# RWKV scan without zero-padded operands, with the gram in a two-bank tile, and modulations computed 512 columns at a time

## The chip, the core and the metric

The kernel runs on one core of one Trainium2 chip. The metric is the device time of one execution in microseconds (us). The profile names the engines PE (TensorE matmuls), PEld (TensorE weight loads), DVE (VectorE), ACT (ScalarE), POOL (GpSimd) and SP (SyncE, which issues all of this kernel's DMAs). "L529" is line 529 of the kernel before.

## The reference

Two layers, each a token mixer and a convolutional FFN, over 1024 latent and 256 context tokens of width 1024. The mixer has four groups of heads; two matter here. The RWKV-7 group is a bidirectional linear recurrence with four heads of 64 in each direction:

```python
def rwkv_scan(r, w, k, v, a, b, state):
    def step(s_mem, inp):
        rt, wt, kt, vt, at, bt = inp
        sa = jnp.einsum('bhvk,bhk->bhv', s_mem, at)
        s_new = s_mem * wt[:, :, None, :] + sa[..., None] * bt[:, :, None, :] + vt[..., None] * kt[:, :, None, :]
        return s_new, jnp.einsum('bhvk,bhk->bhv', s_new, rt)
```

The modulations are `mod = silu_c @ ada_w[l] + ada_b[l]` for two vectors (latent and context): six groups of 1024 columns per layer, each contracted over 1024 rows of weights.

## The kernel before, in words

A layer projects its input, runs Hyena and retention, and then has a stage in which three things run side by side: the RWKV scan (`rwkv` and its helpers), the mLSTM (`mlstm`) and the modulations (`ada_steps`). When all three have ended, `load_wo` brings the output projection's weights, `mix_out` normalises, gates and projects, and the FFN follows. All instructions of the stage are traced in program order and then arranged by a planner that models their times; each engine and the SP queue afterwards run their own lists strictly in order. The trace order is two steps of the scan, then the whole mLSTM with a step of the modulations at each of its 17 or 19 stations, then the rest of the scan.

The scan takes ten steps per layer. A step handles one tile of 128 tokens forward and one backward (index d), each of two chunks of 64 tokens (c), with four heads as two pairs f and two halves q of the 128 partitions.

- `rwkv_prep` (L470 to L542) loads its operands (L479 to L484), computes decays (L492 to L511), scales keys and queries (L514 to L526), forms the gram of keys with queries (L529), masks it into G (L530), copies or transposes its diagonal blocks into NB (L535, L536), and transposes the keys (L540, copied at L541). For the gram, AR holds the queries with zeros in the other head's partitions: a matmul contracts over all 128 partitions and gives 256 columns for both heads.
- `rwkv_inverse` (L545 to L558) inverts 32x32 triangular blocks: LM is a transposed, replicated copy of NB (L550), X starts at L551, and 31 rounds of a multiply (L557) and an add (L558) follow, one half of the columns on POOL, the other on DVE.
- `rwkv_tail` (L561 to L591) transposes X (L565, L569, L571), completes the 64x64 inverse with two batches of 32x32 matmuls (L577 to L586) and writes XT (L570, L590, L591).
- `rwkv_chain` (L594 to L638) is the serial part: for each chunk i and direction d a round of b0 = G V + AR S (L611, L612), U (L614), XT U (L615), its copy into VSA (L617, half on ACT and half on DVE), and the new state (L621, L622, L624). Then come the outputs y (L629, L630) and their copy or sum into YF (L636, L637). SV holds the state in one half of the partitions and the values in the other; V is loaded into VSA and SV both.

`rwkv` calls them so that step s of the chain stands between the inverse and the tail of step s+1, and the prep of step s+2 follows. G and bt have three buffers, AR three, XT, VSA and SV two, LM, X, NB and most of prep's tiles one. PSUM has two banks each for cbank (chain and tail), dbank (gram and key transposes) and mbank (mLSTM and modulations), one for ybank and one for pbank (L492). `ada_steps` works in units of 256 columns, two column groups of 128, whose weights come in four tiles through two buffers; `ada_out` copies the sums to SBUF on DVE (L940), transposes them (L941) and adds the bias (L944). `group_norm` sends YF to the DRAM tensor yw (L659), and `mix_out` reads it back at L1138.

Of the kernel before, what the change touches and what calls it, by code (L numbers as in the profile page):

```python
# [429 lines left out]
def rwkv(K,l,pv,last,p1,p2,p3):  # L430
# [8 lines left out]
    TWA=p1.tile([128,2,2,128],F32,name="TWA"); nc.gpsimd.memset(TWA,0.0)  # L439
# [4 lines left out]
    for a in range(2):  # L444
        r=slice(64,128) if a==0 else slice(0,64); o=slice(0,64) if a==0 else slice(64,128)
# [24 lines left out]
def rwkv_prep(K,C,s):  # L470
    nc=K.nc; act=nc.scalar.activation; tt=nc.vector.tensor_tensor; mm=nc.tensor.matmul; ts=nc.vector.tensor_scalar
    p=C['p']; p3=C['p3']; pv=C['pv']; bank=K.dbank; A=ALU
    rkk=p3.tile([128,2,8,128],F32,tag="rkk",name="rkk")
# [972 lines left out]
```

## Time and profile before

| what | value |
|---|---|
| median of 3 runs | 4259.41 us (4256.86 to 4265.3) |
| the profiled execution's own time | 4269.9 us |
| its span, first to last instruction | 4268.0 us |
| mean granted TensorE clock | 0.940 of full speed |
| busy shares of the span | PE 93%, DVE 63%, ACT 33%, POOL 23% |

The page gives shares over the whole span. The stage of the change is two stretches of it, one per layer, about 770 to 1239 us and 2948 to 3391 us; the long stretches around them are projections and FFN, where PE is busy almost without a break. A busy time of PE counts overlapping modelled durations, so within the stage the starts of its instructions tell more than the share.

### The profile page before, as it was taken

How to read it: one execution, taken by the hardware profiler on the slowest of the kernel's cores; microseconds unless marked ns; L12 is line 12 of the kernel's file. 1: busy time of each engine (PE TensorE's matmuls, PEld its weight loads, DVE VectorE, ACT ScalarE, POOL GpSimd, SP SyncE). 2: the span in 40 equal slices, each digit the busy share in tenths (PEclk: the TensorE clock that was granted, in tenths of full speed). 3: DMA queues.
4: the chain of work that ended last, by engine and by line, in shares of the span. 5: the costliest groups of instructions: out<-in, count | busy, mean ns of one | idle time of the engine just before them, and what ended most of it. 6: DMA issues, size and time to landing. Idle time of an engine off the chain costs nothing.

```text
span 4268.0 us, 65334 instructions
## 1 busy us (share of the span) xinstructions
PE 3956.8 (93%) x24976; PEld 3210.9 (75%) x24976; DVE 2672.2 (63%) x5412; ACT 1416.9 (33%) x2855; POOL 979.7 (23%) x2158
## 2 busy tenths in 40 slices
PE   5999999699979999999997999996899899999998
PEld 3878877566668888888884688885666678888886
DVE  5655665789769444444449555676888684444447
ACT  4433343554344211211123433344544342112121
POOL 3320023466512000000021221024666320000002
PEclk6999999789989999999998999997899699999999
DMA  4235444343343111111113235553332431111112
GB/s 166 74 102 177 149 153 122 112 143 116 122 160 119 45 40 34 41 40 35 37 35 124 82 91 154 169 162 114 122 115 84 136 114 55 48 41 55 45 50 99
DMA packets 477138, 414.16 MB, mean 97 GB/s; under 512 B 48827, under 2 KB 443284, under 8 KB 474010
## 3 DMA queue, kind: packets, MB, share of 16 engines
q1 hardware_dynamic: 476826, 409.99, 31.0%
q8 instruction: 197, 3.23, 0.3%
q14 instruction: 115, 0.94, 0.1%
HBM read 323.65 MB, written 86.25 MB: 96 GB/s over the span
## 4 chain that ended last, share of the span: by engine, by line
PE 52%; DVE 11%; DMA 3%; issue 2%; POOL 1%; ACT 1%; SPq 0%; ACTq 0%; DVEq 0%; POOLq 0%
PE bank L1022 9%; PE bank L1023 9%; PE bank L1024 9%; PE dbank L1022 6%; PE dbank L1023 6%; PE dbank L1024 6%; DVE bst L983 1%; DMA xt<-x 1%; DVE facc L1205 1%; PE bank L186 1%; PE bank L187 1%; DMA wst<-in_w_out 1%; PE dbank L529 0%; DVE facc L1206 0%; DVE facc L1274 0%
## 5 line engine op out<-in xcount | busy, mean ns | idle before, releaser
L1022 PE MATMUL dbank<-uh,wh 128*128 128x512 f32 (+1 forms) x2120 | 765.3, 370 | 8.8 <-ACT tmpB L398 5.7
L1023 PE MATMUL dbank<-ul,wh 128*128 128x512 f32 (+1 forms) x2120 | 761.2, 368 | 0.0
L1016 DVE TENSOR_TENSOR wl<-wst,wh 128x1024 fp32r<-128x1024 f32 x146 | 185.5, 1272 | 491.9 <-ACT wh L1015 367.3
L1024 PE MATMUL dbank<-uh,wl 128*128 128x512 f32 (+1 forms) x2120 | 480.6, 367 | 0.0
L1022 PEld LDWEIGHTS dbank<-uh,wh 128*128 128x128 f32 x2120 | 401.4, 189 | 85.0 <-ACT tmpB L398 6.1
L1023 PEld LDWEIGHTS dbank<-ul,wh 128*128 128x128 f32 x2120 | 401.6, 189 | 68.9 <-issue 1.1
L1024 PEld LDWEIGHTS dbank<-uh,wl 128*128 128x128 f32 x2120 | 365.9, 188 | 70.5 <-issue 1.5
L1264 DVE TENSOR_TENSOR facc<-facc,bank 128x512 f32<-128x512 f32 x324 | 221.8, 686 | 205.1 <-PE bank L1024 205.1
L1022 PE MATMUL bank<-uh,wh 128*128 128x512 f32 (+1 forms) x920 | 334.9, 372 | 4.5 <-ACT uh L1010 4.5
L1233 POOL MEMSET fz<- 128x1 f32 x132 | 7.2, 98 | 1433.6 <-DVE fc L1248 1433.6
L1023 PE MATMUL bank<-ul,wh 128*128 128x512 f32 (+1 forms) x920 | 335.1, 372 | 0.8 <-DVE ul L1011 0.8
L1022 PE MATMUL bank<-wdh,gh 128*128 128x512 f32 x792 | 314.9, 400 | 17.9 <-DVE facc L1278 8.7
L1023 PE MATMUL bank<-wdl,gh 128*128 128x512 f32 x792 | 310.5, 392 | 1.0 <-DVE wdl L1016 1.0
L1024 PE MATMUL bank<-wdh,gl 128*128 128x512 f32 x792 | 248.1, 392 | 0.0
L1015 ACT ACTIVATE wh<-wst 128x1024 fp32r<-128x1024 f32 x146 | 154.8, 1060 | 238.1 <-PE dbank L1023 168.4
L1015 ACT ACTIVATE wdh<-wst 128x1024 fp32r<-128x1024 f32 x46 | 48.8, 1062 | 529.4 <-PE bank L1024 427.7
L558 POOL TENSOR_TENSOR XL<-XL,lt 128x48 f32<-128x48 f32 (+26 forms) x620 | 204.4, 330 | 47.7
L557 POOL TENSOR_TENSOR lt<-LM,XL 128x48 f32<-128x48 f32 (+26 forms) x620 | 187.1, 302 | 119.4 <-ACT XL L551 45.0
L1024 PE MATMUL bank<-uh,wl 128*128 128x512 f32 (+1 forms) x920 | 211.9, 372 | 0.0
L1022 PEld LDWEIGHTS bank<-uh,wh 128*128 128x128 f32 x920 | 174.1, 190 | 36.1 <-ACT uh L1010 5.6
L1023 PEld LDWEIGHTS bank<-ul,wh 128*128 128x128 f32 x920 | 174.2, 189 | 31.9 <-DVE ul L1011 1.7
L1022 PEld LDWEIGHTS bank<-wdh,gh 128*128 128x128 f32 x792 | 149.7, 189 | 59.4 <-DVE facc L1278 14.9
(476 smaller groups left out, 8132.3 us busy)
## 6 DMA issues: line engine op xcount, KB each, us to landing
wst<-in_ffn_w_up SPq DMA_DIRECT2D x88, 512.0 KB
adaw<-in_ada_w SPq DMA_DIRECT2D x160, 256.0 KB
wst<-in_w_in SPq DMA_DIRECT2D x58, 512.0 KB
wst<-in_ffn_w_down SPq DMA_DIRECT2D x46, 512.0 KB
df<-in_c_F SPq DMA_DIRECT2D x10, 1344.0 KB
xt<-x SPq DMA_DIRECT2D x26, 512.0 KB
df<-in_c_I SPq DMA_DIRECT2D x8, 1344.0 KB
rkk<-wrk SPq DMA_DIRECT2D x10, 1024.0 KB
```

Source lines behind the costliest of these rows:

```text
L186: mm(dst_re,F[:,i],pre(slot),start=True,stop=False); mm(dst_re,F[:,i+1],pim(slot),start=False,stop=True)
L187: mm(dst_im,F[:,i],qim(slot),start=True,stop=False); mm(dst_im,F[:,i+2],qre(slot),start=False,stop=True)
L557: e.tensor_tensor(out=t_,in0=LM[:,j,j+1:32].unsqueeze(2).to_broadcast([128,n,m]),in1=X[h][:,j:j+1,0:m].to_broadcast([128,n,m]),op=A.mult)
L558: e.tensor_tensor(out=X[h][:,j+1:32,0:m],in0=X[h][:,j+1:32,0:m],in1=t_,op=A.add)
L983: for h in range(2): nc.vector.bn_stats(out=st[:,h],in_=x[h])
L1015: k.nc.scalar.activation(out=h,in_=st,func=ACTF.Copy)
L1016: k.nc.vector.tensor_tensor(out=lo,in0=st,in1=h,op=ALU.subtract)
L1022: mm(ps,lh,rh,start=(i==0),stop=False)
L1023: mm(ps,lh,rl,start=False,stop=False)
L1024: for i,((lh,ll),(rh,rl)) in enumerate(pairs): mm(ps,ll,rh,start=False,stop=(i==n-1 and more is None))
L1205: for o,i,gg in zip([y[:,h] for h in hs],x,[g[:,h] for h in hs]) if parts else [(y,x,g)]: stt(out=o,in0=i,scalar=m,in1=gg,op0=ALU.subtract ...
L1264: else: tt(out=d,in0=d,in1=ps,op=ALU.add)
```

## The change

The zero halves of AR, TWA and XT go, and with them the memsets that made them. The gram is formed per head from 64 partitions, the two heads into the two banks of one PSUM tile (xbank, one buffer); the key transposes move from dbank to pbank. The state has its own tile S, both halves in one update; V is no longer loaded twice. AR S, XT U and AR S in y become 64x64 matmuls; the identity pass for the state is one 128x128 matmul instead of four. All copies at L591 and L617 are on ACT, the products rho (L601) on POOL. y stands on the partitions of its head, so the copy into YF is one instruction per direction, and the DRAM tensor yw has another order, which `mix_out` undoes with eight small DMAs instead of one. Modulations use a stationary operand padded to 32 columns, units of 512 columns (four column groups) and eight buffers of weights, and one ACT copy of the sums instead of two (four at the start of the program) on DVE. dbank is gone in the stage; `load_rows` uses mbank there.

```diff
-    TWA=p1.tile([128,2,2,128],F32,name="TWA"); nc.gpsimd.memset(TWA,0.0)
+    TWA=p1.tile([128,2,128],F32,name="TWA")
...
-    AR=[p1.tile([128,2,2,2,2,2,64],F32,name="AR%d"%i) for i in range(3)]
-    for t in AR: nc.gpsimd.memset(t[64:128,:,:,:,0],0.0); nc.gpsimd.memset(t[0:64,:,:,:,1],0.0)
-    XT=[p1.tile([128,2,4,128],F32,name="XT%d"%i) for i in range(2)]
+    AR=[p1.tile([128,2,2,2,2,64],F32,name="AR%d"%i) for i in range(3)]
+    XT=[p1.tile([128,2,4,64],F32,name="XT%d"%i) for i in range(2)]
...
-        for X in (VSA,SV):
-            for o,n in PAIR: nc.sync.dma_start(X[r,q,o].rearrange("p d c f e -> p d (c f e)") if o is ALL else X[r,q,o].rearrange("p c f e -> p (c f e)"),K.D['wv'][n,q].rearrange("n p c x -> p n (c x)") if o is ALL else K.D['wv'][n,q].rearrange("p c x -> p (c x)"))
+        r=slice(q*64,q*64+64); X=VSA
+        for o,n in PAIR: nc.sync.dma_start(X[r,q,o].rearrange("p d c f e -> p d (c f e)") if o is ALL else X[r,q,o].rearrange("p c f e -> p (c f e)"),K.D['wv'][n,q].rearrange("n p c x -> p n (c x)") if o is ALL else K.D['wv'][n,q].rearrange("p c x -> p (c x)"))
...
-                o=slice(d*256+ft*128,d*256+ft*128+128); mm(bb[i][:,o],C['W2'][:,o],C['TWA'][:,i,d],start=True,stop=True)
+                r=slice(i*64,i*64+64); o=slice(d*256+ft*128,d*256+ft*128+128); mm(bb[i][:,o],C['W2'][r,o],C['TWA'][r,d],start=True,stop=True)
...
-        for q in range(2):
-            r=slice(q*64,q*64+64)
-            (nc.gpsimd if d==0 else nc.vector).tensor_tensor(out=ar[r,d,:,:,q,0],in0=v4(rkk[r,d,6:8]),in1=Wp[r],op=A.mult)
-            tt(out=ar[r,d,:,:,q,1],in0=v4(rkk[r,d,0:2]),in1=W[r],op=A.mult)
-        for a in range(2): tt(out=bk[:,d,:,:,a],in0=bk[:,d,:,:,a],in1=Wi,op=A.mult)
-        for c in range(2):
-            b=bank()
-            for f in range(2): mm(b[:,f*256:f*256+256],bk[:,d,f,c].rearrange("p a t -> p (a t)"),ar[:,d,f,c].rearrange("p q a t -> p (q a t)"),start=True,stop=True)
-            tt(out=G[:,d,c].rearrange("p f q t -> p (f q) t"),in0=b.rearrange("p (a t) -> p a t",a=4),in1=C['rmask'][:,d].unsqueeze(1).to_broadcast([128,4,128]),op=A.mult)
+        (nc.gpsimd if d==0 else nc.vector).tensor_tensor(out=ar[:,d,:,:,0],in0=v4(rkk[:,d,6:8]),in1=Wp,op=A.mult)
+        tt(out=ar[:,d,:,:,1],in0=v4(rkk[:,d,0:2]),in1=W,op=A.mult)
+        bka=bk[:,d].rearrange("p f c a t -> p (f c) a t"); tt(out=bka,in0=bka,in1=Wi.rearrange("p f c t -> p (f c) t").unsqueeze(2).to_broadcast([128,4,2,64]),op=A.mult)
+        b=K.xbank(); b=[b[:,i] for i in range(2)]
+        for cf in range(4):
+            for q in range(2):
+                r=slice(q*64,q*64+64); c,f=cf//2,cf%2
+                mm(b[q][:,cf*128:cf*128+128],bk[r,d,f,c].rearrange("p a t -> p (a t)"),ar[r,d,f,c].rearrange("p a t -> p (a t)"),start=True,stop=True)
+        for q in range(2): tt(out=G[:,d,:,:,q].rearrange("p c f t -> p (c f) t"),in0=b[q].rearrange("p (a t) -> p a t",a=4),in1=C['rmask'][:,d].unsqueeze(1).to_broadcast([128,4,128]),op=A.mult)
...
-        b=bank()
+        b=K.pbank()
...
-        nc.vector.tensor_copy(out=XT[hi,1,:,lo],in_=bv[hi])
+        act(out=XT[hi,1,:,0:32],in_=bv[hi],func=ACTF.Copy)
...
-        for d in range(2): tt(out=rho[:,i,d],in0=io[:,1,d,:,i^d],in1=(Pn if i else P)['io'][:,0,d,:,d if i else 1-d],op=A.mult)
+        for d in range(2): nc.gpsimd.tensor_tensor(out=rho[:,i,d],in0=io[:,1,d,:,i^d],in1=(Pn if i else P)['io'][:,0,d,:,d if i else 1-d],op=A.mult)
...
-                for r,q in HQ: mm(b0[r,f*64:f*64+64],ar[:,d,f,ch,q,0],SV[:,d,ch,q,f],start=False,stop=True)
+                for q in range(2): mm(b0[H[1-q],f*64:f*64+64],ar[H[q],d,f,ch,0],S[H[q],d,ch,f],start=False,stop=True)
...
-            for f in range(2): mm(b1[:,f*64:f*64+64],XT[:,d,ch*2+f],U[:,f],start=True,stop=True)
+            for f in range(2):
+                for r in H: mm(b1[r,f*64:f*64+64],XT[r,d,ch*2+f],U[r,f],start=True,stop=True)
...
-            act(out=VSA[0:64,d,ch,0],in_=bv[0:64],func=ACTF.Copy); nc.vector.tensor_copy(out=VSA[64:128,d,ch,1],in_=bv[64:128])
+            for r,q in ((H[0],1),(H[1],0)): act(out=VSA[r,d,ch,q],in_=bv[r],func=ACTF.Copy)
...
-                    for r,q in HQ: mm(b2[r,f*64:f*64+64],K.ident[:,r],SV[:,d,ch,q,f],start=True,stop=False)
+                mm(b2,K.ident,S[:,d,ch].rearrange("p f e -> p (f e)"),start=True,stop=False)
...
-                for r,q in HQ: tt(out=SN[r,d,cn,q],in0=bv[r],in1=rho[r,i,d].unsqueeze(2).to_broadcast([64,2,64]),op=A.mult)
+                tt(out=SN[:,d,cn],in0=b2.rearrange("p (f e) -> p f e",f=2),in1=rho[:,i,d].unsqueeze(2).to_broadcast([128,2,64]),op=A.mult)
...
+            for d in range(2):
+                c=i^d
+                for f in range(2):
+                    for q in range(2): mm(y[H[q],d,c,f],G[:,d,c,f,q,64:128],VSA[:,d,c,q,f],start=True,stop=False)
+                    for q in range(2): mm(y[H[q],d,c,f],ar[H[q],d,f,c,1],S[H[q],d,c,f],start=False,stop=True)
...
-    for j in range(G): nc.vector.tensor_copy(out=ab[32*j:32*j+2],in_=ps[32*j:32*j+2,0:n])
+    nc.scalar.activation(out=ab,in_=ps[:,0:n],func=ACTF.Copy)
...
-        for h in range(4):
-            t=pool.tile([128,2,256],F32,tag="adaw",name="adaw",bufs=2); w[u].append(t)
+        for q in range(8):
+            t=pool.tile([128,512],F32,tag="adaw",name="adaw",bufs=8); w[u].append(t)
...
-                for j in range(2): nc.tensor.matmul(ps[32*j:32*j+2,0:128],k.sc[:,q],w[u][q//2][:,q%2,j*128:j*128+128],start=(q==0),stop=(q==7))
+                for j in range(4): nc.tensor.matmul(ps[32*j:32*j+32,0:128],sc[:,q],w[u][q][:,j*128:j*128+128],start=(q==0),stop=(q==7))
...
+            for t in range(2):
+                for c_ in range(2):
+                    for q in range(2): nc.sync.dma_start(yv[c_*64:c_*64+64,t,q],yw[t,c_,q])
...
-        psum(k,cbank=2,ybank=1,pbank=1,dbank=2,mbank=2)
+        psum(k,cbank=2,ybank=1,pbank=1,xbank=-1,mbank=2)
```

## Rows read from the trace of the kernel before

**Rows 1.** The page: its head.
```profile
span 4268.0 us, 65334 instructions
```

**Rows 2.** Windows, both stages: length, busy PE PEld DVE ACT POOL, PEclk, DMA, GB/s.
```profile
770.00:1239.00 469.00, 392.51 (x4570) 293.40 (x4570) 386.38 (x1156) 220.49 (x591) 251.61 (x693) 0.86 0.42 128
2948.00:3391.00 443.00, 367.53 (x4094) 281.34 (x4095) 373.44 (x1095) 204.68 (x572) 249.42 (x689) 0.81 0.37 114
```

**Rows 3.** Source view of L550: ns min/median/max, first to last start; each layer.
```profile
L550 DVE STREAM_TRANSPOSE LM<-NB x10: 1924/1952/1967, 804.5 to 1121.8; 128x1024 f32<-128x1024 f32 x10
...
L550 DVE STREAM_TRANSPOSE LM<-NB x10: 1929/1958/1992, 2984.9 to 3322.0; 128x1024 f32<-128x1024 f32 x10
```

**Rows 4.** Groups, 770 to 1200 us, POOL: count | busy, mean ns | idle before.
```profile
L558 POOL TENSOR_TENSOR XL<-XL,lt 128x52 f32<-128x52 f32 (+26 forms) x310 | 101.1, 326 | 23.8
L557 POOL TENSOR_TENSOR lt<-LM,XL 128x52 f32<-128x52 f32 (+26 forms) x310 | 93.6, 302 | 59.6 <-ACT XL L551 23.1 <-DVE LM L550 13.2
```

**Rows 5.** Timeline, first layer: start, length, engine, line, [idle before <- what ended it].
```profile
944.02 1.95 DVE L550 STREAM_TRANSPOSE LM<-NB 128x1024 f32<-128x1024 f32 x1
...
974.09 1.94 DVE L550 STREAM_TRANSPOSE LM<-NB 128x1024 f32<-128x1024 f32 x1
...
1061.20 0.79 ACT L636 ACTIVATE YF<-ybank 128x128 f32<-128x128 f32 x4 [5.13 <-PE ybank L630]
...
1079.11 1.26 ACT L536 ACTIVATE NB<-G 32x128 f32<-32x128 f32 x4 [2.06 <-DVE G L530]
...
1085.42 1.97 DVE L550 STREAM_TRANSPOSE LM<-NB 128x1024 f32<-128x1024 f32 x1
```

**Rows 6.** Groups by line, 770 to 1200 us, DVE.
```profile
L515 DVE TENSOR_TENSOR bk<-bk,rkk 128x256 f32<-128x256 f32 x40 | 17.8, 477 | 1.6 <-ACT bk L514 1.4
L791 DVE TENSOR_TENSOR NUM<-NUM,dn 128x512 f32<-128x512 f32 x8 | 5.7, 708 | 0.1
L624 DVE TENSOR_TENSOR SV<-cbank,rho 64x128 f32<-64x128 f32 x76 | 21.9, 288 | 13.6 <-PE cbank L622 12.5
L617 DVE COPY VSA<-cbank 64x128 f32<-64x128 f32 x40 | 11.7, 294 | 5.1 <-ACT VSA L617 4.1
L940 DVE COPY ab<-mbank 2x128 f32<-2x128 f32 x46 | 12.8, 279 | 3.8 <-PE mbank L973 3.1
```

**Rows 7.** Timeline of PE: the gram, L492, and a row-tiled matmul of retention.
```profile
710.15 0.72 PE L846 MATMUL bank<-rT 64*128 64x128 f32 x8
...
783.69 1.46 PE L529 MATMUL dbank<-AR,bk 128*128 128x256 f32 x6
784.99 1.05 PE L492 MATMUL pbank<-TWA,W 128*128 128x128 f32 x8
```

**Rows 8.** Timeline of PE: part of y, then of a chain round.
```profile
1060.61 0.29 PE L630 MATMUL ybank<-SV,AR 128*64 128x64 f32 x4
1060.72 0.29 PE L629 MATMUL ybank<-VSA,G 128*64 128x64 f32 x4
...
1081.10 0.34 PE L612 MATMUL cbank<-SV,AR 128*64 128x64 f32 x4
1081.37 0.33 PE L611 MATMUL cbank<-SV,G 64*64 64x64 f32 x4
```

**Rows 9.** Groups, PE, 770 to 1200 us; waits of SP: total, count, longest.
```profile
L973 PE MATMUL mbank<-adaw,sc 128*2 128x128 f32 x736 | 58.3, 293 | 8.2 <-DMA adaw<-in_ada_w 8.0
L492 PE MATMUL pbank<-TWA,W 128*128 128x128 f32 x152 | 23.5, 300 | 17.4 <-ACT ex L497 17.4
...
SPq L966 <- PE mbank L973: 123.0, 54, 10.7
```

**Rows 10.** The first layer's end: source view of L792; timeline of SP and PE.
```profile
L792 DVE TENSOR_TENSOR mV<-NUM x10: 383/420/560, 1020.8 to 1213.8; 128x256 f32<-128x256 f32 x10
...
1216.37 0.47 SPq L1138 DMA_DIRECT2D yt<-yw  x1
...
1238.99 0.77 PE L1022 MATMUL bank<-wo,uh 128*128 128x512 f32 x1 [20.66 <-ACT uh L1157]
```

More of the change, by code (lines that the diff above doesn't have):

```diff
@@ L444, in rwkv @@
     for a in range(2):
-        r=slice(64,128) if a==0 else slice(0,64); o=slice(0,64) if a==0 else slice(64,128)
+        r=slice(a*64,a*64+64); o=slice(64-a*64,128-a*64)
         nc.gpsimd.memset(kas[o,a],-0.5)
@@ L471, in rwkv_prep @@
     nc=K.nc; act=nc.scalar.activation; tt=nc.vector.tensor_tensor; mm=nc.tensor.matmul; ts=nc.vector.tensor_scalar
-    p=C['p']; p3=C['p3']; pv=C['pv']; bank=K.dbank; A=ALU
+    p=C['p']; p3=C['p3']; pv=C['pv']; A=ALU
     rkk=p3.tile([128,2,8,128],F32,tag="rkk",name="rkk")
-    VSA,SV=[p.tile([128,2,2,2,2,64],F32,tag=n,name=n,bufs=2) for n in ("VSA","SV")]
+    VSA=p.tile([128,2,2,2,2,64],F32,tag="VSA",name="VSA",bufs=2)
+    S=p.tile([128,2,2,2,64],F32,tag="SV",name="S",bufs=2)
     f,g=FWT[s],BWT[s]
@@ L606, in rwkv_chain @@
             ch=i^d
-            if s==0 and i==0:
-                for r,q in HQ: nc.gpsimd.memset(SV[r,d,ch,q],0.0)
+            if s==0 and i==0: nc.gpsimd.memset(S[:,d,ch],0.0)
             b=K.cbank(); b0,b1,b2=(b[:,z*128:z*128+128] for z in range(3))
             for f in range(2):
-                for r,q in HQ: mm(b0[r,f*64:f*64+64],G[64-q*64:128-q*64,d,ch,f,q,0:64],SV[64-q*64:128-q*64,d,ch,q,f],start=True,stop=False)
-                for r,q in HQ: mm(b0[r,f*64:f*64+64],ar[:,d,f,ch,q,0],SV[:,d,ch,q,f],start=False,stop=True)
+                for q in range(2): mm(b0[H[1-q],f*64:f*64+64],G[H[q],d,ch,f,q,0:64],VSA[H[q],d,ch,q,f],start=True,stop=False)
+                for q in range(2): mm(b0[H[1-q],f*64:f*64+64],ar[H[q],d,f,ch,0],S[H[q],d,ch,f],start=False,stop=True)
@@ L618, in rwkv_chain @@
             more=i==0 or Pn is not None
             if more:
+                mm(b2,K.ident,S[:,d,ch].rearrange("p f e -> p (f e)"),start=True,stop=False)
                 for f in range(2):
-                    for r,q in HQ: mm(b2[r,f*64:f*64+64],K.ident[:,r],SV[:,d,ch,q,f],start=True,stop=False)
-                    for r,q in HQ: mm(b2[r,f*64:f*64+64],bt[:,d,ch,f,q],VSA[:,d,ch,q,f],start=False,stop=True)
-                bv=b2.rearrange("p (f e) -> p f e",f=2); SN,cn=(SV,1-ch) if i==0 else (Pn['SV'],d)
@@ L624, in rwkv_chain @@
-                for r,q in HQ: tt(out=SN[r,d,cn,q],in0=bv[r],in1=rho[r,i,d].unsqueeze(2).to_broadcast([64,2,64]),op=A.mult)
+                    for q in range(2): mm(b2[H[q],f*64:f*64+64],bt[:,d,ch,f,q],VSA[:,d,ch,q,f],start=False,stop=f==1)
+                SN,cn=(S,1-ch) if i==0 else (Pn['S'],d)
+                tt(out=SN[:,d,cn],in0=b2.rearrange("p (f e) -> p f e",f=2),in1=rho[:,i,d].unsqueeze(2).to_broadcast([128,2,64]),op=A.mult)
         if need_y:
-            yo=lambda q,d,f: yb[q][(i^d)*64:(i^d)*64+64,d*128+f*64:d*128+f*64+64]
@@ L627, in rwkv_chain @@
-            for f in range(2):
-                for q in range(2):
-                    for d in range(2): mm(yo(q,d,f),G[:,d,i^d,f,q,64:128],VSA[:,d,i^d,q,f],start=True,stop=False)
-                    for d in range(2): mm(yo(q,d,f),ar[:,d,f,i^d,q,1],SV[:,d,i^d,q,f],start=False,stop=True)
+            for d in range(2):
[3 more added lines that the diff above has]
+                    for q in range(2): mm(y[H[q],d,c,f],ar[H[q],d,f,c,1],S[H[q],d,c,f],start=False,stop=True)
@@ L631, in rwkv_chain @@
     if need_y:
         for d in range(2):
-            t=tiles[d]; Yv=YF[:,t].rearrange("p (f q) e -> p f q e",q=2)
-            for q in range(2):
-                bb=yb[q][:,d*128:d*128+128].rearrange("p (f e) -> p f e",f=2)
-                if t not in C['seen']: act(out=Yv[:,:,q],in_=bb,func=ACTF.Copy)
-                else: tt(out=Yv[:,:,q],in0=bb,in1=Yv[:,:,q],op=A.add)
+            t=tiles[d]; Yv=YF[:,t]; bb=y[:,d].rearrange("p c f e -> p (c f) e")
+            if t not in C['seen']: act(out=Yv,in_=bb,func=ACTF.Copy)
+            else: tt(out=Yv,in0=bb,in1=Yv,op=A.add)
@@ L927, in ada_setup, with ada_sc @@
     k.modc=k.p_c.tile([128,6,8,2],F32,name="modc")
+def ada_sc(k,pool):
+    s=pool.tile([128,8,32],F32,name="scz"); k.nc.gpsimd.memset(s,0.0); k.nc.gpsimd.tensor_copy(out=s[:,:,0:2],in_=k.sc)
+    return s
 def ada_bias(k,todo,pool):
@@ L1348, in psum @@
     for n,c in pools.items():
-        p=k.psum_es.enter_context(k.tc.tile_pool(name=n,bufs=c,space=bass.MemoryType.PSUM))
-        setattr(k,n,lambda p=p,n=n: p.tile([128,512],F32,tag=n,name=n))
+        p=k.psum_es.enter_context(k.tc.tile_pool(name=n,bufs=abs(c),space=bass.MemoryType.PSUM))
+        setattr(k,n,lambda p=p,n=n,c=c: p.tile([128,512] if c>0 else [128,2,512],F32,tag=n,name=n))
 def layer(k,l,out):
@@ L1414, in tile_backbone @@
         loads=[]
-        ab=pa.tile([128,256],F32,name="ab"); nc.gpsimd.memset(ab,0.0)
+        ab=pa.tile([128,256],F32,name="ab"); sc=ada_sc(k,pa)
         bias=ada_bias(k,[(0,0),(0,1)],pa)
-        for g in range(2): ada(k,0,g,pa,ab,loads,6,bias)
+        for g in range(2): ada(k,0,g,pa,ab,loads,6,bias,sc)
         mc=k.modc[:,0:2].rearrange("p m j s -> p s m j")
```

43 lines of the change are left out of this document (22 added, 21 removed).

## The prediction

> **What bounds the kernel now.** I read the head of the page first [rows 1], then windows for the two stretches in which the edited lines run [rows 2]; the rest of the span is projections and FFN, which the change leaves alone. In neither stretch does one engine fill the time. DVE is closest (386 of 469 us, 82%, and 373 of 443, 84%), PE's busy time is inflated by overlapping durations, ACT and POOL stand near half. So the next view is one that shows a pace. There is one LM per step of the scan, and its starts lie (1121.8 - 804.5)/9 = 35.3 us apart in the first layer and (3322.0 - 2984.9)/9 = 37.5 us in the second [rows 3]. What sets this pace?
>
> Two loops are nearly equal. **Loop one is POOL's half of the inverse**: 31 multiplies and 31 adds a step, in series, 62 x 0.314 = 19.5 us busy, and with the idle time before them (59.6 + 23.8 us over ten steps) 27.8 us a step [rows 4]. There is one LM, so the next transpose cannot start before POOL has read the last one. The shortest period shown is 974.09 - 944.02 = 30.1 us [rows 5]; that is about what this loop costs when nothing else is late. **Loop two is the ring of three G buffers**: LM of step 5 at 974.09; the copy of y that ends chain 5, and so frees G, at 1061.20; the copies into NB of step 8 at 1079.11; LM of step 8 at 1085.42 [rows 5]. That is 111.3 us for three steps, 37.1 a step, of which the prep after the release takes 24 us. Both loops cross DVE, whose queue is in order and which also holds all of mLSTM's work. What a step takes from DVE therefore sets how late each link of the loops is served.
>
> **The change part by part, per step. DVE:** the 256-column products are now done in fewer, larger instructions. Before there are 14 (L515 4, L524 on DVE 2, L525 4, L526 4); at 477 ns, the mean of L515 [rows 6], 6.7 us. After there are four of 512 columns (L515 over both directions for each operand, L526 over both operands for each direction) and three of 256 over all 128 partitions (L524's on DVE, L525's two). With 0.71 for 512 columns (L791) [rows 6] that is 4 x 0.71 + 3 x 0.477 = 4.3: -2.4 us. L624 goes from 8 instructions over 64 partitions to 4 over 128: at 288 ns, -1.15. L617's half on DVE leaves, 4 x 0.294 = -1.18, and so do L591's two copies, priced like L617, -0.58. L601's four small products go to POOL: they cannot cost DVE more than L617's 0.29 each, and I count -0.6. Sum -5.9 a step, -59 a layer. L940 adds -13 us in the first layer, since its 46 copies become ACT's [rows 6]. DVE in the first stretch would fall by 72 of 386 us.
>
> **PE:** Six passes of the gram's 256 columns take 1.30 us from start to start (783.69 to 784.99) [rows 7], 0.217 each, so a step's 16 take 3.5. After there are 32 passes of 128 columns from 64 partitions into two banks. Eight such of retention (L846) take 0.72 us, where L492's eight over 128 partitions take 1.05 [rows 7]: by that ratio 32 x 0.109 x 0.69 = 2.4, and if two always run together 16 x 0.109 = 1.7. I take 1.9, nearer to the second since the pairs are issued side by side: -1.6. In a chain round the start of four passes lies 0.11 us from the next group when the shape stays (1060.61 to 1060.72), 0.27 when it changes (1081.10 to 1081.37) [rows 8]. L611 and L612 make 16 such groups a step and now have one shape: 16 x 0.27 = 4.3 becomes 16 x 0.15, between the two, = 2.4. L615 gives about -0.9, the identity pass and L622 +0.5 (one change of shape each round more), both estimates by the same two gaps. In y the shapes now alternate: 16 x (0.27 - 0.11) = +2.5, or nothing if they are not put strictly in turn. L973's 736 instructions of 58.3 us [rows 9] become half, since four column groups share a pass's time: about -2 a step. In all -3.4 a step, of which only the rounds lie on a loop.
>
> **ACT and POOL:** ACT gains 4 copies at L617 and two at L591, +1.7 a step, and has the idle time for it [rows 2]; if that cover went, ACT's queue would hold U and bt, both in loop two. POOL loses a launch of L524 (-0.7, an estimate by half of two 64-partition instructions) and gains rho, between 0 and 4 x 0.33 = 1.3 (a small element product no dearer than L558 [rows 4]); I take 1.1, so +0.4. If rho stands ahead of the inverse in POOL's queue it is on loop one, and that is in the price.
>
> **What is free:** the memsets are at the stage's start, beside DMAs; V's second load saves two DMAs a step where both directions go together and four elsewhere, some 60 in all, which SP does not lack: its long waits are those of the modulations' weights, 123.0 us over 54 waits for PE to release a buffer [rows 9], and eight buffers instead of two take most of these away. What queues behind them on SP are the loads for prep. The prologue's modulations wait for their weights from DRAM in any case.
>
> **The sum.** Over three steps DVE has 3 x 5.9 = 18 us less to do. I take half of it to lie on the ring, since the other half falls where DVE waits or serves mLSTM: 9 us of 111.3, or 3 a step. The bounds: 0, if POOL alone sets the pace; 35.3 - 30.1 = 5.2 and 37.5 - 30.1 = 7.4, if both loops come down to the shortest period seen. In the second layer I take 4, since the pace is slower there and the granted clock lower (0.81 against 0.86 of full speed [rows 2], means over its two levels of 1.2 and 2.4 GHz), so that PE's savings count for more. First layer: 9 x -3 = -27; second: 9 x -4 = -36. The first LM comes 34 us into the stretch [rows 2, 3], behind two preps in series that each lose 2.4 us of DVE: of the 4.8 I take 3 in each layer. After the last LM, tail and chain run without an overlapping prep: four rounds whose PE part shrinks by half a us each, and -2 from the tail and y, in all -4 a layer. Against this: yw is read back by eight DMAs instead of one. At 0.47 us an issue [rows 10] this is +3.3 us of SP's queue, and in the first layer it stands ahead of the weights that PE needs after its gap; +3 there, hidden in the second. Total -27 - 36 - 6 - 8 + 3 = -74. The profiled execution took 4269.9 us, so 4196 for one like it; it lies 10.5 above the median of the runs, 4259.4, and against that I forecast 4185.
>
> **A rule to weigh.** L611 reads 64 partitions and writes 64, two row tiles side by side into one bank. Its four passes take 0.33 us, and those of L612, which read all 128 partitions, 0.34 [rows 8]: the row shows no cost for two row tiles in one bank. The Trainium skill, TensorEngine Tiling (Array Packing), section Restrictions and Gotchas, says that different row tiles cannot access the same PSUM bank at the same time. By that rule the 64x64 matmuls would run one after the other and the sum would be rival 3's; the trace so far does not agree, with 0.33 against 0.34 us.
>
> **Rivals.**
> 1. **POOL's inverse stays the pace.** For it: 27.8 us a step [rows 4] of 35.3, and the change adds rho there. Then the starts and ends remain, -14, and some of the second layer, where other work is late too, -15: 4230. Against it: the ring's 37.1 [rows 5] is longer than POOL's loop. Chance 0.17.
> 2. **Both loops come down to the shortest period and mLSTM ends early.** 9 x -5.2 and 9 x -7.4 = -113, and part of PE's 20.66 us of idle time at the first layer's end [rows 10] closes, which follows mLSTM's last tile at 1213.8; I take 10 of it. With -14 for starts and ends about -140, 4120. Chance 0.15.
> 3. **Row tiles of one bank exclude each other.** L612, L615 and y's second half lose their pairing: 12 groups x 0.23 = +2.8 us a step, half of it on the path, 1.4 x 20 = +28: -46, 4213. Chance 0.07.
> 4. **Slower: PE stands behind a single buffer.** xbank is one tile and pbank one bank, and PE takes its list in order. L492's wait for pbank shows the price: 17.4 us over ten steps, 1.74 a use [rows 9]. The gram of the second direction must wait for both masks of the first (2 x 0.71 by the 512-column row, more if DVE is late), and the key transposes for ACT's copy of bt. With three such waits, each 1.7, PE loses 5 us a step; chain rounds and mLSTM's matmuls are queued behind it. It decides from 74/20 = 3.7 us a step on the path; at 5 the sum is 20 x 5 - 74 = +26: 4285. Chance 0.10.
> 5. **Nothing to measure**: the planner puts the same waits elsewhere. 0.2% or 8.5 us is about what a measurement of this kernel tells from no change. Chance 0.03.
>
> The forecast has 0.48. The range runs from 4115, just below rival 2, to 4250; above lie rival 4, rival 5 and the edge of rival 1. Faster by over 0.2%: 0.48 + 0.17 + 0.15 + 0.07, less 0.03 for a forecast that shrinks to nothing: 0.84. Same 0.06, slower 0.10.
>
> **What would show it.** Right: LM starts about 32 to 33 us apart; the groups L515 and L624 with half the DVE time; L973 with half the instructions and no long wait of SP for PE; the gram near 2 us a step. Wrong: PE's idle time led by waits for the masks (DVE) or the copy bt (ACT) before the gram or L540, which is rival 4; POOL busy without a gap from one LM to the next, which is rival 1; L612's passes 0.2 us apart, which is rival 3.

## The result: slower, and the profile after

The changed kernel takes 4312.2 us (median of 4 runs, 4298.2 to 4321.4) against 4261.0 for the kernel before: ratio 1.0117, 95% interval 1.0085 to 1.0150. That is 51 us more where 74 less were forecast. The profiled execution has a span of 4316.3 us. Its lines are shifted against the kernel before: L514, L528, L540, L549, L556 and L623 are what L515, L529, L541, L550, L557 and L624 were, L976 is L973, L1025 is L1022.

The two stages again, from about 6 us after the end of retention to PE's first matmul of the output projection, in the columns of [rows 2]:

```profile
811.00:1277.00 466.00, 382.70 (x4651) 293.35 (x4652) 325.18 (x880) 237.21 (x651) 267.70 (x721) 0.75 0.39 123
2987.00:3443.00 456.00, 365.14 (x4178) 283.00 (x4178) 308.65 (x841) 227.53 (x632) 259.26 (x715) 0.68 0.33 105
```

DVE did lose its work, 61 us in the first stage and 65 in the second [rows 2]. But the time did not follow: 466 us against 469 in the first, 456 against 443 in the second. And the first begins 41 us later, at 811 instead of 770. So two questions are open: what delays everything ahead of the stage, and why does the stage not get shorter? The pace of the scan answers to [rows 3], source view of L549:

```profile
L549 DVE STREAM_TRANSPOSE LM<-NB x10: 1901/1948/1995, 837.1 to 1219.2; 128x1024 f32<-128x1024 f32 x10
...
L549 DVE STREAM_TRANSPOSE LM<-NB x10: 1902/1941/1965, 3014.8 to 3384.7; 128x1024 f32<-128x1024 f32 x10
```

It is (1219.2 - 837.1)/9 = 42.5 us a step and 41.1 in the second layer, where 35.3 and 37.5 were measured before and 32 to 33 were forecast. The parts that the prediction priced one by one, groups by line from 811 to 1240 us (to be read beside [rows 4, 6, 9]):

```profile
L514 DVE TENSOR_TENSOR bk<-bk,rkk 128x512 f32<-128x512 f32 x20 | 14.2, 712 | 1.5 <-ACT bk L513 1.5
...
L623 DVE TENSOR_TENSOR S<-cbank,rho 128x128 f32<-128x128 f32 x34 | 9.4, 278 | 5.8 <-PE cbank L621 5.7
...
L556 POOL TENSOR_TENSOR lt<-LM,XL 128x52 f32<-128x52 f32 (+26 forms) x299 | 98.8, 331 | 82.1 <-DVE LM L549 52.2 <-DVE AX L570 4.1 <-ACT XL L550 4.1
...
L976 PE MATMUL mbank<-adaw,scz 128*32 128x128 f32 x768 | 31.2, 313 | 0.0
```

The durations were right: 712 ns for 512 columns (0.71 taken), 278 ns for the state's update over 128 partitions (288 taken). POOL's line is the one to look at. Its idle time in front of the inverse that a late LM ended was 13.2 us [rows 4], and is 52.2 now. So POOL does not set the pace (rival 1); it waits for LM, which comes late. PE's own part, timeline of the second layer for a chain round and the gram, of the first for y:

```profile
3099.13 0.28 PE L610 MATMUL cbank<-S,AR 64*64 64x64 f32 x4
3099.24 0.28 PE L609 MATMUL cbank<-VSA,G 64*64 64x64 f32 x4
3099.36 0.28 PE L610 MATMUL cbank<-S,AR 64*64 64x64 f32 x4
...
3192.96 1.16 PE L528 MATMUL xbank<-AR,bk 64*128 64x128 f32 x16
3194.05 0.66 PE L539 MATMUL pbank<-ident,bk 128*128 128x128 f32 x4
...
1027.66 0.33 PE L629 MATMUL ybank<-S,AR 64*64 64x64 f32 x4
1027.92 0.34 PE L628 MATMUL ybank<-VSA,G 128*64 128x64 f32 x4
1028.18 0.33 PE L629 MATMUL ybank<-S,AR 64*64 64x64 f32 x4
```

Groups of one shape start 0.11 to 0.12 us apart and y's alternating shapes 0.26, as taken; a direction's gram takes 1.09 us, so 2.2 a step where 1.9 was taken. The 64x64 matmuls lie on two row tiles of one bank, write the two halves of its partitions, and start as close together as those of one shape did in [rows 8]. By the 0.217 us of a pass of 256 columns [rows 7], four passes of 64 columns would take 0.22 us one after the other (an estimate); they take half. The Trainium skill, TensorEngine Tiling (Array Packing), section Restrictions and Gotchas, says that different row tiles cannot access the same PSUM bank simultaneously; this trace does not agree, and rival 3 falls with it.

### The profile page after: what moved, and what is told of

Read it like the earlier page. It is cut to its first block, busy times and chain, and to the rows that moved or that the text cites. A ratio compares the mean times of both kernels' runs of the same rounds, so it can differ in the third digit from the quotient of the medians.

```text
span 4316.3 us, 65313 instructions
## 1 busy us (share of the span) xinstructions
PE 3971.6 (92%) x25140; PEld 3236.0 (75%) x25140; DVE 2525.1 (59%) x4874; ACT 1451.6 (34%) x2975; POOL 991.1 (23%) x2199
## 4 chain that ended last, share of the span: by engine, by line
PE 67%; DVE 10%; POOL 10%; issue 5%; DMA 4%; ACT 3%; SPq 1%; POOLq 0%; ACTq 0%; DVEq 0%
PE bank L1026 9%; PE bank L1025 9%; PE bank L1027 9%; PE dbank L1025 9%; PE dbank L1026 8%; PE dbank L1027 8%; POOL XL L557 4%; POOL lt L556 4%; PE bank L186 1%; PE bank L187 1%; DVE bst L986 1%; DMA xt<-x 1%; PE bank L849 1%; DVE LM L549 1%; PE mbank L758 1%
## 5 line engine op out<-in xcount | busy, mean ns | idle before, releaser
L1025 PE MATMUL dbank<-uh,wh 128*128 128x512 f32 (+1 forms) x2120 | 766.0, 370 | 3.6 <-ACT tmpB L407 2.1
L1025 PEld LDWEIGHTS dbank<-uh,wh 128*128 128x128 f32 x2120 | 401.8, 190 | 82.6 <-ACT ztok L1117 4.6
L1025 PE MATMUL bank<-uh,wh 128*128 128x512 f32 (+1 forms) x920 | 334.5, 371 | 3.3 <-ACT uh L1013 3.3
L1025 PE MATMUL bank<-wdh,gh 128*128 128x512 f32 x792 | 315.7, 401 | 14.6 <-DVE facc L1285 4.9
L556 POOL TENSOR_TENSOR lt<-LM,XL 128x48 f32<-128x48 f32 (+26 forms) x620 | 201.1, 324 | 155.9 <-DVE LM L549 93.7
L557 POOL TENSOR_TENSOR XL<-XL,lt 128x48 f32<-128x48 f32 (+26 forms) x620 | 214.3, 346 | 46.0
L1025 PEld LDWEIGHTS bank<-uh,wh 128*128 128x128 f32 x920 | 173.8, 189 | 34.5 <-ACT uh L1013 4.1
L1025 PEld LDWEIGHTS bank<-wdh,gh 128*128 128x128 f32 x792 | 149.6, 189 | 57.3 <-DVE facc L1285 11.5
```

Of the source, the lines that this page charges most:

```text
L556: e.tensor_tensor(out=t_,in0=LM[:,j,j+1:32].unsqueeze(2).to_broadcast([128,n,m]),in1=X[h][:,j:j+1,0:m].to_broadcast([128,n,m]),op=A.mult)
L557: e.tensor_tensor(out=X[h][:,j+1:32,0:m],in0=X[h][:,j+1:32,0:m],in1=t_,op=A.add)
L1025: mm(ps,lh,rh,start=(i==0),stop=False)
```

## The experiments

Each ratio below is against the kernel before as measured beside the run (4258 to 4263 us); runs that were not measured side by side are compared by their ratios.

**The front.** In the kernel before, retention ends at 763.4 us, in the changed one at 804.3 (last matmul of each). Nothing there was edited. But the first matmul of Hyena's filters, and the load of its matrix, had moved. SP and PE of the kernel before, then of the changed one:

```profile
21.21 0.38 SPq L268 DMA_DIRECT2D fft<-in_c_FT  x1
...
29.53 1.93 PE L273 MATMUL bank<-fft,fw 33*64 33x512 f32 x4 [1.44 <-DMA fft<-in_c_FT]
```

```profile
90.28 0.29 SPq L268 DMA_DIRECT2D fft<-in_c_FT  x1
...
94.06 1.93 PE L273 MATMUL bank<-fft,fw 33*64 33x512 f32 x4
```

The padded operand of the modulations is a new tile, 1 KB per partition, in the pool of the program's start. Theory A was that it pushes that pool onto the memory in which the filters' pools are placed next, so that the filters must wait until x is transposed. Four kernels went together. The first adds nothing but an idle tile to the kernel before; the second and third take memory back in two different ways; the fourth also splits the change.

```diff
         ab=pa.tile([128,256],F32,name="ab"); nc.gpsimd.memset(ab,0.0)
+        pad=pa.tile([128,8,32],F32,name="padt"); nc.gpsimd.memset(pad,0.0)
```

> The kernel before with one unused tile of 1 KB per partition in the pool of the program's start, nothing else. Theory A (the padded operand of the modulations, 1 KB, moves the memory of the filters of layer 0 onto that of the loads of x, so that the filters wait until x is transposed): the filters' first matmul moves from 29.5 us to about 90, retention of layer 0 ends some 40 us later as in the changed kernel (764 to 805), and the time is about 4261 + 41 = 4302, ratio 1.010. Theory B (the loss in front of the stage comes from the new matmuls and copies themselves): no change, 4261, ratio 1.000.

Measured: 4308.5 us against 4261.7, ratio 1.0106 (1.0085 to 1.0128). One idle KB costs 47 us. SP and PE of this kernel:

```profile
88.24 0.29 SPq L268 DMA_DIRECT2D fft<-in_c_FT  x1
...
92.20 1.93 PE L273 MATMUL bank<-fft,fw 33*64 33x512 f32 x4
```

The second run is the changed kernel with `ada` and `ada_out` of the start as before (`k.sc` instead of `sc`, no `scz`):

> The changed kernel with the modulations of the program's start as before (two-column operand, no 1 KB tile, four copies on DVE). Theory A: the first layer's front is as before, retention ends near 764 us instead of 805, and 41 of the 51 us are back: about 4271, ratio 1.002. Theory C (the scan's stage itself makes the loss and the front only shifts it): no more than 10 us back, 4302 or more, ratio 1.010.

Measured: 4270.6, ratio 1.0018 (1.0006 to 1.0030).

```diff
-        for g in range(2): ada(k,0,g,pa,ab,loads,6,bias,sc)
+        for g in range(2): ada(k,0,g,pa,ab,loads,5,bias,sc)
```

> The changed kernel with five buffers of weights instead of six at the program's start (4 KB less), all new matmuls kept. Theory A: the filters start early again and the time is about 4271 to 4275 (some us for the buffer), ratio 1.003. Theory B: no gain, 4312 or more, since nothing but memory changed, ratio 1.012.

Measured: 4264.5, ratio 1.0010 (0.9998 to 1.0023), with the filters early again:

```profile
17.17 0.37 SPq L268 DMA_DIRECT2D fft<-in_c_FT  x1
...
22.95 3.67 PE L273 MATMUL bank<-fft,fw 33*64 33x512 f32 x4
```

So theory A holds. Theory B, that the new arithmetic of the start does it, does not, and neither does theory C: 42 us came back in the second run. The size of the pool decides. (That the two share addresses is inferred from this; the trace shows no addresses.) The price is not paid where the filters wait: with them later, the projections end some 11 us earlier in the changed kernel. It is paid at 700 to 805 us. Hyena's last long convolution then ends at 607.5 instead of 560.1 us. Retention's first 80 matmuls (L820, now L817) come at 701 to 725 us, after the last projection at 694; before they stood between the projections, at 636 to 708. What is left of retention then runs with PE at the lower of its two levels, 1.2 GHz. Windows of 20 us, kernel before, then changed kernel:

```profile
740.00:760.00 20.00, 20.00 (x153) 17.71 (x153) 9.72 (x23) 8.88 (x20) 3.37 (x3) 1.00 0.12 41
```

```profile
740.00:760.00 20.00, 19.66 (x85) 17.80 (x86) 6.30 (x12) 5.35 (x11) 3.42 (x5) 0.50 0.09 36
760.00:780.00 20.00, 19.40 (x88) 17.36 (x86) 5.03 (x11) 5.19 (x11) 1.46 (x2) 0.50 0.08 27
780.00:800.00 20.00, 19.07 (x84) 16.71 (x84) 6.74 (x17) 4.38 (x9) 1.04 (x1) 0.50 0.04 14
```

The fourth run has `ada_steps` as before too, so that only the scan is changed:

> The change of the scan alone: all modulations as before. Theory D (what is lost in the second layer's stage, 13 us from the end of retention to the first matmul of the projection, comes from the scan): like the run with only the start's modulations put back, about 4271, ratio 1.002. Theory E (it comes from the units of 512 columns with their eight loads ahead of the scan's loads on SP): about 4271 - 13 - some us in the first layer, 4255, ratio 0.998.

Measured: 4270.2, ratio 1.0021 (1.0004 to 1.0039). Theory D fits and E does not: the change of the scan alone, without the new modulations, gains nothing.

**The stage: three suspects.** With 46 us explained (1.0117 against 1.0010), the rest of the change was worth nothing instead of -74. The base is now the changed kernel with five buffers (4264.5 us); its LM starts:

```profile
L549 DVE STREAM_TRANSPOSE LM<-NB x10: 1903/1928/1982, 811.0 to 1178.6; 128x1024 f32<-128x1024 f32 x10
...
L549 DVE STREAM_TRANSPOSE LM<-NB x10: 1872/1934/1972, 2978.4 to 3329.3; 128x1024 f32<-128x1024 f32 x10
```

40.8 and 39.0 us a step. The suspects were POOL's queue (theory P), PE's granted clock, which had fallen (Q), and ACT's additional copies (R).

```diff
-        for d in range(2): nc.gpsimd.tensor_tensor(out=rho[:,i,d], ...
+        for d in range(2): tt(out=rho[:,i,d], ...
```

> The changed kernel with five buffers at the start (4264.5 us) and the products rho on DVE as before. Theory P (POOL's queue paces the scan: rho waits there up to 24.6 us for DVE's S L623, with the inverse behind it): the waits of POOL for S, 30.5 us in the first layer, go and the time falls by 15 to 40, 4225 to 4250, ratio 0.992 to 0.997. Theory Q (PE's clock and PE's list pace it): no change, 4260 to 4268, ratio 1.000 to 1.002.

Measured: 4286.0, ratio 1.0061 (1.0044 to 1.0078): slower, neither theory's number.

```diff
-            nc.gpsimd.tensor_tensor(out=ru[32:40] ...
+            nc.vector.tensor_tensor(out=ru[32:40] ...
```

> The changed kernel with five buffers and mLSTM's product mRU (L755, 20 a layer at 1.1 us, which wait on POOL for PE's L758) on DVE. Theory P: POOL loses 22 us of work and the waits in front of it in the first layer, and the time falls by 15 to 40, 4225 to 4250, ratio 0.992 to 0.997. Theory Q: no change, ratio 1.000 to 1.002; slower if DVE is late for L758.

Measured: 4268.6, ratio 1.0019 (1.0008 to 1.0029). No gain; theory P falls.

```diff
+            for _ in range(4): mm(b[:,384:512],K.ident,K.ident,start=True,stop=True)
             U=p.tile([128,2,64],F32,tag="U%d"%d,name="U")
```

> The changed kernel with five buffers and four extra 128x128 matmuls of the identity in each chain round, into columns of cbank that nobody reads: 16 a step, 3.5 us of PE at the higher clock, about what the change took away. Theory Q (with less work PE is granted its lower clock, and PE is then the pace): granted clock in the two stages up from 0.79 and 0.72 towards 0.86 and 0.81, time down by 10 to 30, 4235 to 4255, ratio 0.994 to 0.998. Theory P: PE's extra work lies beside POOL's inverse or in the rounds, time up by 0 to 40, ratio 1.001 to 1.010.

Measured: 4280.7, ratio 1.0050 (1.0034 to 1.0065). The granted clock did rise; windows of the base, then of this run:

```profile
778.00:1234.00 456.00, 363.44 (x4651) 281.27 (x4651) 322.14 (x880) 235.49 (x649) 262.74 (x720) 0.79 0.40 125
2945.00:3385.00 440.00, 349.04 (x4179) 271.86 (x4180) 305.92 (x841) 228.29 (x633) 258.25 (x715) 0.72 0.35 109
```

```profile
782.00:1249.00 467.00, 401.07 (x4970) 318.37 (x4970) 323.80 (x880) 237.14 (x650) 259.98 (x720) 0.84 0.39 123
2954.00:3402.00 448.00, 373.45 (x4498) 299.07 (x4498) 306.40 (x841) 228.18 (x634) 254.16 (x715) 0.81 0.34 106
```

From 0.79 to 0.84 and from 0.72 to 0.81 (means over 1.2 and 2.4 GHz), nearly the 0.86 and 0.81 of the kernel before, and the stages became 11 and 8 us longer. The time is theory P's and not Q's, but this run alone does not separate them: the extra matmuls stand in the round ahead of U, and ACT's waits for PE in front of U rose from 11.9 to 37.0 us in the first stage. What the clock gave may be hidden behind that. A later run decides it, which gains at the low clock.

```diff
-        act(out=XT[hi,1,:,0:32],in_=bv[hi],func=ACTF.Copy)
+        nc.vector.tensor_copy(out=XT[hi,1,:,0:32],in_=bv[hi])
...
-            for r,q in ((H[0],1),(H[1],0)): act(out=VSA[r,d,ch,q],in_=bv[r],func=ACTF.Copy)
+            act(out=VSA[H[0],d,ch,1],in_=bv[H[0]],func=ACTF.Copy); nc.vector.tensor_copy(out=VSA[H[1],d,ch,0],in_=bv[H[1]])
```

> The changed kernel with five buffers and the copies of L591 and half of L617 on DVE as before. Theory R (ACT, which has the transposed inverse, U, VSA, bt and mLSTM's copies in one queue, is late in the rounds): time down by 10 to 20, 4245 to 4255, ratio 0.996 to 0.999. Theories P and Q: no change, 4260 to 4268, ratio 1.000 to 1.002.

Measured: 4276.4, ratio 1.0036 (1.0020 to 1.0052). Theory R falls. Three of these four edits make the kernel 11 to 22 us slower than its base (by the ratios), and only for the third can a mechanism be named; the planner arranges the whole stage anew for every edit, so single differences of this size are not read further.

**The stage: the order.** In the base's first layer, mLSTM's last tile comes at 1150 us and the scan's last sum at 1225; before it was 1214 and 1200. So mLSTM seems to have had DVE's free time. If the trace order is what gives it precedence, tracing the scan first should turn this round.

```diff
-                    for _ in range(2): next(scan)
+                    for _ in range(10): next(scan)
```

> The changed kernel with five buffers, with all ten steps of the scan traced ahead of mLSTM instead of two, so that the planner puts the scan first. Theory O (the time that the scan's smaller work set free was taken by mLSTM and the modulations, which stand ahead of eight of its steps in the trace: mLSTM ends 76 and 109 us before the scan does): the LM starts come 29 to 33 us apart as in the first two steps, instead of 40.8 and 39.0, and the time falls by 50 to 120, 4145 to 4215, ratio 0.973 to 0.990. Theory S (the queues are full by the sum of the three parts' work): no gain, mLSTM then ends as much later, 4255 to 4290.

Measured: 4383.3, ratio 1.0286 (1.0267 to 1.0305).

> The kernel before with all ten steps of the scan traced ahead of mLSTM. Theory O: its LM starts come nearer than 35.3 and 37.5 us, but DVE is fuller by 59 us a layer, so it gains less than the changed kernel does: 4210 to 4260, ratio 0.988 to 1.000. Theory S: no gain or a loss, 4260 to 4300.

Measured: 4484.1, ratio 1.0531 (1.0498 to 1.0565).

```diff
-                    mlstm(k,l,GT,last,side)
+                    def both(i):
+                        side(i)
+                        if i%2: next(scan,None)
+                    mlstm(k,l,GT,last,both)
```

> The changed kernel with five buffers, with the eight later steps of the scan traced at every second station of mLSTM. Theory O: between the two orders, 20 to 80 us less than 4264, 4185 to 4245, ratio 0.982 to 0.996. Theory S: 4255 to 4290.

Measured: 4295.9, ratio 1.0082 (1.0057 to 1.0106).

> The kernel before with the eight later steps of the scan traced at every second station of mLSTM. Theory O: 0 to 40 us less, 4220 to 4262, ratio 0.991 to 1.000. Theory S: 4260 to 4300.

Measured: 4280.7, ratio 1.0049 (1.0030 to 1.0067). Theory O falls: each other order is slower for both kernels. With the scan first, mLSTM ends last in both layers (in the first at 1291 us against 1193 for the scan, and at 1339 against 1159 in the kernel before); with the steps spread out it ends last in the first layer only, by 18 and 34 us. Yet the two runs with the scan first hold the clue, since nothing stands in the scan's way there. LM starts of the changed kernel, then of the kernel before, first layer:

```profile
L549 DVE STREAM_TRANSPOSE LM<-NB x10: 1902/1948/1969, 815.4 to 1134.4; 128x1024 f32<-128x1024 f32 x10
```

```profile
L550 DVE STREAM_TRANSPOSE LM<-NB x10: 1899/1936/1993, 799.3 to 1094.0; 128x1024 f32<-128x1024 f32 x10
```

35.4 against 32.7 us a step: with precedence, and with less work, the changed scan is the slower one. That points to a loop of the scan itself. (PE's granted clock was lower too in these stretches, 0.64 against 0.73; what that adds is not shown.)

**The stage: pbank.** The copies that end prep's two uses of PSUM show which. In the kernel before (L497 empties pbank after L492; L541 empties dbank after the key transposes), ACT's timeline:

```profile
953.92 0.58 ACT L497 ACTIVATE ex<-pbank 128x512 f32<-128x512 f32 x1
957.63 0.60 ACT L541 ACTIVATE bt<-dbank 128x512 f32<-128x512 f32 x1
964.04 0.60 ACT L541 ACTIVATE bt<-dbank 128x512 f32<-128x512 f32 x1 [2.40 <-PE dbank L540]
```

The L497 at 953.92 is that of step 7, the two copies bt are step 5's, and step 6's are still to come: prep's first part runs more than a step ahead of its last. In the base of these runs:

```profile
967.28 0.60 ACT L540 ACTIVATE bt<-pbank 128x512 f32<-128x512 f32 x1 [1.42 <-PE pbank L539]
971.98 0.60 ACT L540 ACTIVATE bt<-pbank 128x512 f32<-128x512 f32 x1
975.81 0.59 ACT L496 ACTIVATE ex<-pbank 128x512 f32<-128x512 f32 x1
```

Here each prep's first matmuls come after the bt copies of the prep before it, in all ten steps of both layers: pbank is one bank, and it is handed out in trace order. That this takes prep's lead is the second theory to be called B. Four kernels tested it.

```diff
-        b=K.xbank(); b=[b[:,i] for i in range(2)]
+        b=[K.gbank() for i in range(2)]
...
-        b=K.pbank()
+        b=K.gbank()
...
-        psum(k,cbank=2,ybank=1,pbank=1,xbank=-1,mbank=2)
+        psum(k,cbank=2,ybank=1,pbank=1,gbank=2,mbank=2)
```

> The changed kernel with five buffers, the gram's two banks as two tiles of a pool of two, and the key transposes in that pool instead of pbank. Theory B (one pbank for the decays' matmuls L491 and the key transposes makes each prep wait for the bt copy of the prep before it, so prep no longer runs ahead): L491 of a prep comes before the transposes of the one before, LM starts 33 to 36 us apart instead of 40.8 and 39.0, and the time falls by 20 to 60, 4205 to 4245, ratio 0.987 to 0.997. Theory S (the sum of all queues holds the stage): no change, 4258 to 4275, ratio 1.000 to 1.003.

Measured: 4226.4, ratio 0.9930 (0.9912 to 0.9948), faster than the kernel before. ACT's timeline has the lead again (the L496 is step 7's, the two copies are step 5's), and the LM starts are 36.7 and 36.6 us apart:

```profile
979.83 0.58 ACT L496 ACTIVATE ex<-pbank 128x512 f32<-128x512 f32 x1
989.77 0.59 ACT L540 ACTIVATE bt<-gbank 128x512 f32<-128x512 f32 x1
999.74 0.59 ACT L540 ACTIVATE bt<-gbank 128x512 f32<-128x512 f32 x1
```

```profile
L549 DVE STREAM_TRANSPOSE LM<-NB x10: 1900/1947/2001, 816.4 to 1146.4; 128x1024 f32<-128x1024 f32 x10
...
L549 DVE STREAM_TRANSPOSE LM<-NB x10: 1900/1930/1977, 2966.1 to 3295.2; 128x1024 f32<-128x1024 f32 x10
```

Its two stages, in the columns of [rows 2]:

```profile
782.00:1217.00 435.00, 371.36 (x4650) 289.61 (x4650) 319.04 (x880) 232.29 (x648) 259.44 (x720) 0.79 0.42 131
2929.00:3354.00 425.00, 356.44 (x4179) 277.49 (x4180) 310.21 (x841) 223.42 (x631) 253.39 (x715) 0.74 0.37 112
```

The time came back while the granted clock stayed near the base's 0.79 and 0.72: the stages are 34 and 18 us shorter than in the kernel before, which had 0.86 and 0.81 [rows 2]. So the lower clock is not what held the base back (theory Q).

The next run moves the transposes alone, into the gram's buffer (`b=K.xbank()[:,0]`):

> The changed kernel with five buffers and only the key transposes moved, from pbank to a tile of xbank. Theory B: prep runs ahead again, but the second direction's gram waits for the first's bt copy in the one buffer of xbank: 10 to 40 less, 4225 to 4255, ratio 0.991 to 0.999. Theory S: no change, ratio 1.000 to 1.003.

Measured: 4289.2, ratio 1.0072 (1.0060 to 1.0084): slower than the base. Prep does run ahead again (step 7's L496 at 1002.35 us, before step 5's first bt copy at 1006.59), but the LM starts are 41.4 and 40.2 us apart. With one two-bank buffer, the second direction's gram now waits for the first's masks, transposes and bt copy in turn; PE's waits for the masks ahead of the transposes are 12.7 us in the first stage. Prep's lead is worth nothing if the same chain is tied elsewhere.

```diff
-        b=bank()
+        b=K.pbank()
         for c in range(2):
             for f in range(2):
                 nc.tensor.transpose(
```

> The kernel before with one word changed: the key transposes in pbank instead of dbank. Theory B: prep loses its lead, LM starts 37 to 41 us apart instead of 35.3 and 37.5, and the time rises by 20 to 60, 4280 to 4320, ratio 1.005 to 1.014. Theory S: no change, 4255 to 4268, ratio 0.999 to 1.002.

Measured: 4271.7, ratio 1.0033 (1.0021 to 1.0045), LM starts 36.6 and 38.0 us apart. One word makes the kernel before slower, by 13 us rather than the 20 to 60 expected, and the pace misses the expected 37 to 41 us in the first layer. Yet the lead is gone: in both layers each L497 comes after both bt copies of the step before it. So what a lost lead costs depends on the kernel; why it costs this one so little is not shown.

> The changed kernel with five buffers, all steps of the scan traced ahead of mLSTM, gram and key transposes in a pool of two one-bank tiles (against 4383 us with them in xbank and pbank). Theory B: LM starts 29 to 32 us apart, under the 32.7 of the kernel before with the scan first, instead of 35.4 and 37.3, and the time falls by 30 to 60. Theory R (the rounds on PE and ACT, L617 and tail, set the scan's pace): no change in the pace.

Measured: 4366.6, ratio 1.0246 (1.0228 to 1.0264), LM starts (1123.9 - 816.1)/9 = 34.2 and 33.8 us apart. The pace is 1.2 and 3.5 us better than with pbank, and 17 us of the time are back where 30 to 60 were expected. The pace is not under the 32.7 of the kernel before; part of the scan's own lengthening is not explained by this.

The last two separate what the combined edit did. The first moves the gram and leaves the transposes in pbank:

> The changed kernel with five buffers and the gram's two banks as two tiles of a pool of two; the key transposes stay in pbank. Theory B (pbank is the cause: each prep's first matmul waits for the bt copy of the prep before): no gain, 4255 to 4272, ratio 0.999 to 1.003, LM starts 39 to 41 us apart. Theory X (the one two-bank buffer of the gram is the cause): 4220 to 4240, ratio 0.991 to 0.996, as with both moved.

Measured: 4270.6, ratio 1.0028 (1.0018 to 1.0039), LM starts 40.4 and 39.6 us apart: no gain, as theory B expected. What brings the time back is the transposes out of pbank, in a place where they tie nothing else. The second adds a third buffer of VSA (`bufs=3`) to the faster version:

> The version with gram and transposes in a pool of two (4226 us), with three buffers of VSA instead of two. Theory V (SP's wait for VSA's buffer holds up the loads behind it, and through them the next prep): the wait goes, LM starts 33 to 35 us apart, time 4195 to 4215, ratio 0.985 to 0.990. Theory W (prep runs ahead as it is; the pace is the inverse, the tail and the rounds in their queues): no change, 4220 to 4235, ratio 0.991 to 0.995.

Measured: 4249.2, ratio 0.9970 (0.9959 to 0.9982): 17 us worse than without, by the ratios. The LM starts are 36.9 and 37.3 us apart, and SP's waits at VSA's load (L483) only shrank, from 27.6 to 18.2 us in the first stage. Theory V's gain does not come, and theory W's number is not met either; why a third buffer makes it slower is not shown. The version with gbank and two buffers of VSA stays the best one.

## Why the prediction was wrong

By its own steps, and against 4261:

- **"The prologue's modulations wait for their weights from DRAM in any case."** This edit was costed at nothing, and it cost 46 to 47 us, nearly all of the 51. The instructions were indeed free. What was not looked at is the tile that they need: 1 KB in a pool whose memory the next pools reuse. No row of the trace before shows that a pool has no room to grow; it had to be asked of every tile that the change adds.
- **"9 x -3" and "9 x -4", the step pace.** It rose by 7.2 and 3.6 us a step. Rival 4 named the place, one bank pbank and the key transposes in it, but priced it as PE standing 1.7 us at each use. PE's wait for bt's copy was only 3.0 us in the first stage. The price lies elsewhere: a single buffer that is handed out in trace order ties the first operation of one prep to the last of the prep before. With it untied the change gains: 0.9930 against 1.0010 for the base is 34 us. In the kernel before, the same tie cost 13 us only.
- **The ring.** With the transposes out of pbank the pace is 36.7 and 36.6, so 1 us faster in the second layer and 1.4 slower in the first, not 3 to 4 faster. The step that failed is "I take half of it to lie on the ring", 9 us of 111.3. DVE was relieved (61 us of the 72), but the pace did not use it; mLSTM came earlier, its last tile in the first layer at 1168 instead of 1214 us [rows 10]. The gain then came at the stage's end: from the last LM to the projection 71 us instead of 117 in the first layer, 59 instead of 69 in the second, where -4 was forecast for each. With gbank the parts add up: +13 and -8 from the paces, -46 and -10 at the ends, +12 from retention in the first layer, which ends at 775.5 us, are -39; the profiled executions took 4229.1 and 4269.9 us.
- **Starts.** -3 each was forecast; in the first layer it is 41 us from the end of retention to the first LM with gbank and 41 before.
- **PE's terms** held: the gram 2 x 1.09 = 2.2 a step (1.9 taken), rounds and y by the two gaps. L973's instructions did not halve, 768 passes remain; their time did, since four of them share it: 31.2 against 58.3 us. SP's waits for the buffers of weights shrank from 123.0 us in all to 54.0.
- **Rivals.** 1 (POOL the pace): no, POOL waits for LM. 2 (the loops at their best): no. 3 (row tiles): no. 4 (slower, a single buffer): the place right, the mechanism and price not; that its 4285 is the forecast nearest to 4312 is luck, since most of the loss is the memory's. The chance of 0.10 for slower was too low, since it was worked out from one mechanism and the memory was none of the cases.

What stays open: why the changed scan, untied and traced first, still needs 34 us a step where the kernel before needs 32.7 (at a granted clock of 0.63 against 0.73 in the first layer), and why retention in the first layer ends 8 to 22 us later in most runs with the changed scan. In the base, PE's granted clock is 0.71 from 740 to 760 us and 0.50 from 760 to 780 while retention finishes, where the kernel before had 1.00 at 740 to 760; what makes it fall there is not shown. The copies and rho were tried with mLSTM beside them only. A kernel with gbank and the start's modulations as before was not tried.

## What to carry to other kernels

Count bytes as well as instructions: a new tile of 1 KB in a pool can order two parts of a program that shared no data, and an idle tile of that size is a cheap test of it. Before moving an operation into another pool's buffer, write down which first and last uses the buffer then ties together, and look how far ahead the first one ran; a lost lead can cost more than the wait that it shows as (34 us here, against 3.0 us of waits). When a stage holds several independent parts, work taken from one engine can speed up another part than the one meant; ask which part ends last.

## What the runs showed of the hardware

Less work for PE went with a lower granted clock: 0.79 and 0.72 in the stages of the base, 0.86 and 0.81 in the kernel before. Full matmuls that nobody reads raised it to 0.84 and 0.81 and the kernel became 17 us slower, while the version with gbank gained 34 us at 0.79 and 0.74. A lower clock can be the sign of a PE with less to do and not the cause of a longer stage.

Two 64x64 matmuls on different row tiles of one bank, writing different halves of its partitions, started as close together as those on two column groups, groups of four passes 0.11 to 0.12 us apart at the higher level.
